# A quarter of the experts' gate and up weights multiplied as whole float32, with the output scaling on ScalarE and the factor row on GpSimd

## The chip, the cores and the metric

The kernel runs on one core of a Trainium2 chip. The metric is the device time of one execution in microseconds (us). Lower is better.

## The reference

The program is a stack of two blocks on 1024 tokens of width 1024. The first block holds a layer of dilated attention beside a gated scan and a layer of gated scans. The second holds a mixer and, last, a layer of 16 experts in which each expert chooses its tokens. The change touches only the experts:

```python
def expert_choice_ffn(h, router_w, w_gate, w_up, w_down):
    b, T, D = h.shape
    cap = EC_CAPACITY * T // N_EXPERTS
    aff = jax.nn.softmax(jnp.einsum('btd,de->bte', h.astype(F32), router_w.astype(F32)), axis=-1)
    gate, idx = lax.top_k(jnp.swapaxes(aff, 1, 2), cap)
    xe = jax.vmap(lambda hb, ib: hb[ib])(h, idx)
    hid = jax.nn.silu(jnp.einsum('becd,edf->becf', xe, w_gate)) * jnp.einsum('becd,edf->becf', xe, w_up)
    ye = jnp.einsum('becf,efd->becd', hid, w_down) * gate[..., None].astype(h.dtype)
    return jax.vmap(lambda ib, yb: jnp.zeros((T, D), yb.dtype).at[ib.reshape(-1)].add(yb.reshape(-1, D)))(idx, ye)
...
        x = x + m_lat[5][:, None] * expert_choice_ffn(h_lat, router_w[l], exp_w_gate[l], exp_w_up[l], exp_w_down[l])
```

With a capacity of 2, 1024 tokens and 16 experts, `cap` is 128 tokens. An expert's three weight matrices are 1024x512, 1024x512 and 512x1024 in float32. `m_lat[5]` is a row of 1024 factors, the same for every token; `gate` is a number per token and expert.

## The kernel before

Large products are made as three products of a reduced float32 type, `float32r`. A float32 operand is split into `hi` (its copy in float32r, by ScalarE, called ACT in the profile) and `lo` (what is left, by a subtraction on VectorE, DVE, or on GpSimd, POOL). `mm3` (L134 to L141) then issues hi x hi (L139), hi x lo (L140) and lo x hi (L141) into one bank of PSUM on TensorE (PE).

`experts` (L2002) goes through the 16 experts. For each one:

- `gather` (L2025) finds the 128 tokens by small products with a one-hot matrix, and fetches their rows with an indirect DMA that GpSimd issues (`xe`, L2041).
- `hidden` (L2049) turns the rows with eight transposes on TensorE (L2055), splits the result into `xeh` and `xel` (L132 on ACT and L133 on DVE, four chunks of 128 rows at a time), and multiplies with the gate and the up weights.
- `down` (L2071) turns and splits the hidden values (`hidh`, `hidl`), multiplies with the down weights, scales by `gate` (a number per token) and by `m5` (the factor row) in one DVE instruction per half of 512 columns (L2086), and adds the result to `accd` in DRAM with an indirect DMA from GpSimd (L2088, experts 0 to 13). The last two experts' results stay on the chip and are added by matmuls.

Each weight matrix comes in four units of 128x1024 float32 (512 KB) through `units` (L2009): a DMA from the SyncE queue into `eraw` (27 buffers in all), `ehi` by ACT (L2017), `elo` by DVE (L2019) or by POOL (L2021). `ehi` and `elo` have four buffers each. POOL makes `elo` of every unit of expert 0 and, for experts 1 to 14, of the fourth unit of each matrix; DVE makes the others. In the gate and up matrices a unit holds two chunks of 128 rows, in the down matrix one.

```python
if u < 3 and e > 0 or e == 15:
    nc.vector.tensor_sub(lo, raw, hi.bitcast(F32))
else:
    nc.gpsimd.tensor_tensor(lo, raw, hi.bitcast(F32), op=ALU.subtract)
```

The loop computes `hidden` of expert e ahead of `down` of expert e-1. What order the instructions have on each engine is decided by a scheduler when the program is built, which interleaves the two; on the chip each engine takes its instructions in that order.

## Time and profile before

| | us |
|---|---|
| three runs of the kernel | 3703.40, 3707.62, 3709.96 (median 3707.62) |
| the profiled execution, its own time | 3706.74 |
| its span, first to last instruction | 3704.5 |
| mean granted TensorE clock, share of full speed | 0.933 |
| PE busy | 3335.8 (90%) |
| DVE busy | 2592.7 (70%) |
| ACT busy | 1600.5 (43%) |
| POOL busy | 1445.3 (39%) |

Busy time is the time in which at least one instruction of the engine was running; matmuls overlap, so a busy PE can still run below its best rate. PEld is the loading of the stationary operand. A row of the trace names a source line, an engine, an operation and `out<-in`, with the number of instructions after an x. "idle before" is the time that the engine stood still ahead of these instructions, and what ended it. The experts run from about 3296 us to the end of the span; the tanh of their hidden values (L2067), one per expert, comes first at 3305.03 and last at 3654.20 us.

### The profile page before, as it was taken

How to read it: one execution, taken by the hardware profiler on the slowest of the kernel's cores; microseconds unless marked ns; L12 is line 12 of the kernel's file. 1: busy time of each engine (PE TensorE's matmuls, PEld its weight loads, DVE VectorE, ACT ScalarE, POOL GpSimd, SP SyncE). 2: the span in 40 equal slices, each digit the busy share in tenths (PEclk: the TensorE clock that was granted, in tenths of full speed). 3: DMA queues.
4: the chain of work that ended last, by engine and by line, in shares of the span. 5: the costliest groups of instructions: out<-in, count | busy, mean ns of one | idle time of the engine just before them, and what ended most of it. 6: DMA issues, size and time to landing. Idle time of an engine off the chain costs nothing.

```text
span 3704.5 us, 59873 instructions
## 1 busy us (share of the span) xinstructions
PE 3335.8 (90%) x21896; PEld 2717.0 (73%) x21896; DVE 2592.7 (70%) x5580; ACT 1600.5 (43%) x3332; POOL 1445.3 (39%) x1431
## 2 busy tenths in 40 slices
PE   7998998999979999999999999688996889748887
PEld 6886786766758888879798977566775877536665
DVE  4776664346685767976767685679995555578887
ACT  3343333544424545445545441354433331225565
POOL 4556673000041334333334331723215562335544
PEclk9998999999999999999999999788996879869999
DMA  5223244252352212111112234234337555678994
GB/s 179 78 83 95 86 134 136 79 184 88 91 170 66 70 63 57 51 56 46 46 49 65 64 135 154 76 90 130 113 117 175 119 150 177 212 210 291 302 331 161
DMA packets 373986, 461.04 MB, mean 124 GB/s; under 512 B 150419, under 2 KB 280723, under 8 KB 373692
## 3 DMA queue, kind: packets, MB, share of 16 engines
q1 hardware_dynamic: 359852, 407.93, 35.3%
q0 software_dynamic: 13840, 49.29, 4.4%
q8 instruction: 173, 2.83, 0.3%
q14 instruction: 121, 0.99, 0.1%
HBM read 357.57 MB, written 104.27 MB: 125 GB/s over the span
## 4 chain that ended last, share of the span: by engine, by line
PE 60%; DVE 16%; issue 8%; DMA 7%; POOL 4%; ACT 3%; SPq 1%; DVEq 0%; POOLq 0%; ACTq 0%
PE mm L139 12%; PE mm L140 12%; PE mm L141 11%; PE a L247 2%; DVE elo L2019 2%; PE o L225 1%; DVE cacc L1141 1%; PE a L402 1%; PE a L141 1%; PE a L140 1%; PE f L1099 1%; PE o L276 1%; POOL aw L962 1%; PE a L139 1%; PE a L251 1%
## 5 line engine op out<-in xcount | busy, mean ns | idle before, releaser
L116 POOL TENSOR_TENSOR wlo<-wraw,whi 128x1024 fp32r<-128x1024 f32 (+1 forms) x131 | 328.2, 2510 | 518.3 <-ACT whi L115 496.0
L2017 ACT CAST ehi<-eraw 128x1024 fp32r<-128x1024 f32 x192 | 200.5, 1050 | 147.2 <-PE a L141 101.8
L139 PE MATMUL mm<-x1h,whi 128*128 128x512 f32 x576 | 237.4, 412 | 7.6 <-DVE q L621 3.8
L140 PE MATMUL mm<-x1l,whi 128*128 128x512 f32 x576 | 234.9, 408 | 3.0 <-DVE x1l L133 3.0
L141 PE MATMUL mm<-x1h,wlo 128*128 128x512 f32 x576 | 234.7, 407 | 0.0
L139 PE MATMUL mm<-whi,x1h 128*128 128x256 f32 x768 | 222.4, 290 | 0.0
L2019 DVE TENSOR_TENSOR elo<-eraw,ehi 128x1024 fp32r<-128x1024 f32 x138 | 198.2, 1470 | 32.6 <-ACT ehi L2017 32.4
L141 PE MATMUL mm<-whi,x1l 128*128 128x256 f32 x768 | 219.9, 287 | 0.0
L140 PE MATMUL mm<-wlo,x1h 128*128 128x256 f32 x768 | 219.9, 287 | 0.0
L115 ACT CAST whi<-wraw 128x1024 fp32r<-128x1024 f32 (+1 forms) x131 | 136.0, 1040 | 165.1 <-PE mm L140 90.4
L2021 POOL TENSOR_TENSOR elo<-eraw,ehi 128x1024 fp32r<-128x1024 f32 x54 | 139.6, 2591 | 158.1 <-ACT ehi L2017 135.3
L139 PE MATMUL mm<-whi,xh 128*128 128x256 f32 x640 | 184.9, 289 | 0.0
L140 PE MATMUL mm<-wlo,xh 128*128 128x256 f32 x640 | 183.9, 288 | 0.5 <-POOL wlo L116 0.5
L141 PE MATMUL mm<-whi,xl 128*128 128x256 f32 x640 | 183.4, 287 | 0.0
L139 PE MATMUL mm<-x2h,whi 128*128 128x512 f32 x400 | 166.4, 416 | 6.5 <-ACT cu L1130 3.5
L139 PE MATMUL mm<-whi,yin 128*128 128x512 f32 x352 | 148.6, 425 | 22.3 <-DVE z L820 13.9
L140 PE MATMUL mm<-x2l,whi 128*128 128x512 f32 x400 | 164.7, 412 | 0.0
L141 PE MATMUL mm<-x2h,wlo 128*128 128x512 f32 x400 | 163.8, 410 | 0.8 <-POOL wlo L116 0.8
L139 PE MATMUL mm<-xh,whi 128*128 128x512 f32 x336 | 138.9, 413 | 19.8 <-ACT whi L115 16.6
L239 POOL TENSOR_TENSOR u_qh<-u_qa,facX 128x256 f32<-128x256 f32 x64 | 71.4, 1115 | 202.1 <-DVE u_qa L236 170.9
L139 PEld LDWEIGHTS mm<-whi,x1h 128*128 128x128 f32 x768 | 146.9, 191 | 1.1
L962 POOL TENSOR_SCALAR aw<-aw,ac 128x128 f32<-128x128 f32 x256 | 116.3, 470 | 80.2 <-DMA aw<-in_ada_w_dram 32.5
(755 smaller groups left out, 10700.9 us busy)
## 6 DMA issues: line engine op xcount, KB each, us to landing
eraw<-in_we_gate_dram SPq DMA_DIRECT2D x64, 512.0 KB
eraw<-in_we_up_dram SPq DMA_DIRECT2D x64, 512.0 KB
eraw<-in_we_down_dram SPq DMA_DIRECT2D x64, 512.0 KB
yin<-yd POOLq DMA_DIRECT2D x29, 1024.0 KB, 8.5
aw<-in_ada_w_dram SPq DMA_DIRECT2D x96, 256.0 KB
yd<-y_hl SPq DMA_DIRECT2D x80, 256.0 KB
wraw<-in_w_dram SPq DMA_DIRECT2D x25, 512.0 KB
wraw<-in_w_out_dram SPq DMA_DIRECT2D x24, 512.0 KB
```

The lines of the kernel that those rows point to most:

```text
L115: nc.scalar.copy(hi[:, :sz], raw[:, :sz])
L116: nc.gpsimd.tensor_tensor(lo[:, :sz], raw[:, :sz], hi[:, :sz].bitcast(F32), op=ALU.subtract)
L139: nc.tensor.matmul(ps, sh, mh, start=first and i == 0, stop=False)
L140: nc.tensor.matmul(ps, sh, ml, start=False, stop=False)
L141: nc.tensor.matmul(ps, sl, mh, start=False, stop=last and i == n - 1)
L225: nc.tensor.matmul(up[:, :Vd], kdT[:, i * P:(i + 1) * P], V[:, gi, :], start=True, stop=True)
L239: nc.gpsimd.tensor_tensor(v3(qh, 32), v3(qa, 32), bcast(fqh, nck, 32), op=ALU.mult)
L247: nc.tensor.matmul(ap[:, o:o + P], w(kt, 0, P), w(qt, 0, P), start=True, stop=True)
L962: nc.gpsimd.tensor_scalar(w[:, k], w[:, k], at(k), 0.0, op0=ALU.mult, op1=ALU.add)
L2017: nc.scalar.copy(hi, raw)
L2019: nc.vector.tensor_sub(lo, raw, hi.bitcast(F32))
L2021: nc.gpsimd.tensor_tensor(lo, raw, hi.bitcast(F32), op=ALU.subtract)
```

## The change

Of every gate and every up matrix the fourth unit (chunks 6 and 7 of 8) is no longer split. `raw` itself is the moving operand of one plain float32 matmul per chunk, against a float32 copy of the tokens' chunks 6 and 7 (`xew`). The down matrices stay as they were. For experts 0 to 13 the scaling by `gate` moves from DVE to ACT (two activations that read PSUM), and the product with the factor row `m5` becomes an instruction of its own on POOL, ahead of the indirect DMA that adds the result to `accd`.

```diff
--- before.py
+++ after.py
@@ -2006,14 +2006,18 @@
     nc, I = g.nc, g.I
     turns = cycle(rps)
 
-    def units(blk, e, k, n):
+    def units(blk, e, k, n, plain=0):
+
         out = []
         for u in range(4):
             rp, bufs = next(turns)
             raw = rp.tile([P, 1024], F32, name="eraw", tag="eraw", bufs=bufs)
+            nc.sync.dma_start(raw.rearrange("p (k n) -> p k n", n=n), blk[:, u * k:(u + 1) * k, :])
+            if u >= 4 - plain:
+                out += [raw[:, i * n:(i + 1) * n] for i in range(k)]
+                continue
             hi = wp.tile([P, 1024], F32R, name="ehi", tag="ehi", bufs=4)
             lo = wp.tile([P, 1024], F32R, name="elo", tag="elo", bufs=4)
-            nc.sync.dma_start(raw.rearrange("p (k n) -> p k n", n=n), blk[:, u * k:(u + 1) * k, :])
             nc.scalar.copy(hi, raw)
             if u < 3 and e > 0 or e == 15:
                 nc.vector.tensor_sub(lo, raw, hi.bitcast(F32))
@@ -2021,6 +2025,14 @@
                 nc.gpsimd.tensor_tensor(lo, raw, hi.bitcast(F32), op=ALU.subtract)
             out += [(hi[:, i * n:(i + 1) * n], lo[:, i * n:(i + 1) * n]) for i in range(k)]
         return out
+
+    def product(ps, sta, mov):
+
+        whole = [i for i, m in enumerate(mov) if not isinstance(m, tuple)]
+        parts = [i for i, m in enumerate(mov) if isinstance(m, tuple)]
+        g.mm3(ps, [sta[i] for i in parts], [mov[i] for i in parts], last=False)
+        for i in whole:
+            nc.tensor.matmul(ps, sta[i], mov[i], start=False, stop=i == whole[-1])
 
     def gather(e):
 
@@ -2049,19 +2061,24 @@
 
         xh = pool.tile([P, 8, P], F32R, name="xeh", tag="xeh", bufs=2)
         xl = pool.tile([P, 8, P], F32R, name="xel", tag="xel", bufs=2)
+        xw = pool.tile([P, 2, P], F32, name="xew", tag="xew", bufs=2)
         for c0 in range(0, 8, 4):
             tr = g.psum("tr")
             for i in range(4):
                 nc.tensor.transpose(tr[:, i * P:(i + 1) * P], xe[:, (c0 + i) * P:(c0 + i + 1) * P], g.ident)
+            t3 = tr.rearrange("p (c t) -> p c t", t=P)
+            m = min(4, 6 - c0)
             with g.up():
-                g.split(xh[:, c0:c0 + 4], xl[:, c0:c0 + 4], tr.rearrange("p (c t) -> p c t", t=P))
-        sta = [(xh[:, k], xl[:, k]) for k in range(8)]
-        wg = units(I["we_gate"][e], e, 2, 512)
+                g.split(xh[:, c0:c0 + m], xl[:, c0:c0 + m], t3[:, :m])
+                if c0 == 4:
+                    nc.scalar.copy(xw, t3[:, 2:4])
+        sta = [(xh[:, k], xl[:, k]) for k in range(6)] + [xw[:, k] for k in range(2)]
+        wg = units(I["we_gate"][e], e, 2, 512, 1)
         pg = g.psum("a")
-        g.mm3(pg, sta, wg)
-        wu = units(I["we_up"][e], e, 2, 512)
+        product(pg, sta, wg)
+        wu = units(I["we_up"][e], e, 2, 512, 1)
         pu = g.psum("a")
-        g.mm3(pu, sta, wu)
+        product(pu, sta, wu)
         hid = pool.tile([P, 512], F32, name="hid", tag="hid", bufs=2)
         with g.up():
             nc.scalar.activation(hid, pg, AF.Tanh, scale=0.5)
@@ -2083,8 +2100,12 @@
             hs = slice(half * 512, (half + 1) * 512)
             pd = g.psum("o")
             g.mm3(pd, [(hh[:, k], hl[:, k]) for k in range(4)], [(h[:, hs], l[:, hs]) for h, l in wd])
-            nc.vector.scalar_tensor_tensor(y[:, hs], pd, gate, m5[:, hs], op0=ALU.mult, op1=ALU.mult)
+            if e < 14:
+                nc.scalar.activation(y[:, hs], pd, AF.Copy, scale=gate)
+            else:
+                nc.vector.scalar_tensor_tensor(y[:, hs], pd, gate, m5[:, hs], op0=ALU.mult, op1=ALU.mult)
         if e < 14:
+            nc.gpsimd.tensor_tensor(y, y, m5, op=ALU.mult)
             nc.gpsimd.indirect_dma_start(out=accd, out_offset=bass.IndirectOffsetOnAxis(ap=idx, axis=0), in_=y,
                                          in_offset=None, bounds_check=T - 1, compute_op=ALU.add)
             return
```

What the scheduler makes of it is shown at three places. The first is POOL in the middle of the experts, about one expert long. `xe<-h2d,idx` is the gather of an expert's rows, `accd<-ye,idx` the indirect add. Before:

```order
L2088 DMA accd<-ye,idx 1024x1024
L2041 DMA xe<-h2d,idx 128x1024
L2021 TENSOR_TENSOR elo<-eraw,ehi 128x1024 x3
L2088 DMA accd<-ye,idx 1024x1024
L2041 DMA xe<-h2d,idx 128x1024
```

and with the change:

```order
L2025 TENSOR_TENSOR elo<-eraw,ehi 128x1024
L2108 TENSOR_TENSOR ye<-ye,m_32846 128x1024
L2109 DMA accd<-ye,idx 1024x1024
L2053 DMA xe<-h2d,idx 128x1024
L2025 TENSOR_TENSOR elo<-eraw,ehi 128x1024
```

Between two gathers three subtractions have become one, that of the down matrix, and the product of `ye` with the factor row (L2108) stands ahead of each indirect add.

The second place is ACT late in the experts, over one expert, from the tanh (`hid<-a`) to the next. Before:

```order
L2067 ACTIVATE hid<-a 128x512
L2017 CAST ehi<-eraw 128x1024 x9
L132 CAST xeh<-tr 128x512 x2
L2017 CAST ehi<-eraw 128x1024 x2
L132 CAST hidh<-tr 128x512
L2017 CAST ehi<-eraw 128x1024
L2067 ACTIVATE hid<-a 128x512
```

and with the change:

```order
L2084 ACTIVATE hid<-a 128x512
L2021 CAST ehi<-eraw 128x1024 x6
L2104 ACTIVATE ye<-o,gate 128x512 x2
L132 CAST xeh<-tr 128x512
L132 CAST xeh<-tr 128x256
L2074 COPY xew<-tr 128x256
L2021 CAST ehi<-eraw 128x1024 x4
L2084 ACTIVATE hid<-a 128x512
L132 CAST hidh<-tr 128x512
L2021 CAST ehi<-eraw 128x1024 x5
L2104 ACTIVATE ye<-o,gate 128x512 x2
```

The twelve casts of weight units have become ten, and the two scalings of `ye` (L2104), which need the whole down product, stand ahead of the split of the next expert's tokens.

The third place is PE at the end of one expert's up product, with the change only; `a` is the bank of the gate or up product and `o` that of the down product.

```order
L139 MATMUL a<-ehi,xeh 128x512
L140 MATMUL a<-elo,xeh 128x512
L141 MATMUL a<-ehi,xel 128x512
L2035 MATMUL a<-eraw,xew 128x512 x2
L139 MATMUL o<-ehi,hidh 128x512
L140 MATMUL o<-elo,hidh 128x512
L141 MATMUL o<-ehi,hidl 128x512
```

The two float32 matmuls of the unsplit unit (L2035) close the product, where before six matmuls of L139 to L141 stood.

## Rows read from the trace of the kernel before

**Rows 1.** Stretches of the expert stage: busy time of each engine, clock, DMA.

```profile
core 0: us, PE busy (x) PEld busy (x) DVE busy (x) ACT busy (x) POOL busy (x), PEclk, DMA share, GB/s
3303.70:3353.10 49.40, 38.55 (x172) 29.55 (x171) 40.78 (x42) 27.16 (x32) 30.72 (x14) 0.90 0.71 243
3353.10:3477.40 124.30, 103.55 (x453) 79.31 (x453) 96.29 (x108) 71.45 (x78) 71.10 (x25) 0.90 0.90 289
3477.40:3654.20 176.80, 157.04 (x721) 121.25 (x721) 157.31 (x168) 116.24 (x129) 90.16 (x39) 0.97 0.86 289
```

**Rows 2.** Waits in 3300 to 3665 us: total, times, longest us.

```profile
PE a L140 <- POOL elo L2021: 15.8, 4, 5.9
PE a L140 <- DVE elo L2019: 13.0, 6, 4.6
PE a L141 <- DVE xel L133: 12.1, 7, 2.3
```

**Rows 3.** Waits of SyncE's DMA queue from 3170 us: total, times, longest us.

```profile
SPq L2016 <- DVE elo L2019: 132.9, 88, 6.9
```

**Rows 4.** Timeline around 3400 us: start, us, engine, line.

```profile
3396.01 4.72 POOL L2088 DMA_INDIRECT accd<-ye,idx  x1 [1.69 <-DVE gate L2045]
...
3401.03 4.40 POOL L2041 DMA_INDIRECT xe<-h2d,idx  x1 [0.31 <-issue]
...
3405.46 2.35 POOL L2021 TENSOR_TENSOR elo<-eraw,ehi 128x1024 fp32r<-128x1024 f32 x1
...
3407.86 0.79 PE L140 MATMUL a<-elo,xeh 128*128 128x512 f32 x1 [4.88 <-POOL elo L2021]
```

**Rows 5.** Stretches right behind the three longest such waits, columns as in rows 1.

```profile
3407.86:3412.25 4.39, 4.39 (x11) 3.46 (x11) 0.69 (x1) 1.62 (x2) 0.69 (x1) 0.51 1.04 371
3434.32:3439.50 5.18, 5.18 (x12) 4.12 (x13) 0.97 (x2) 2.09 (x2) 1.47 (x1) 0.50 0.99 364
3461.15:3466.80 5.65, 5.65 (x13) 4.46 (x14) 0.69 (x1) 2.03 (x2) 1.95 (x1) 0.50 0.82 293
```

**Rows 6.** Timeline of the early experts around 3335 us.

```profile
3333.06 7.02 POOL L2021 TENSOR_TENSOR elo<-eraw,ehi 128x1024 fp32r<-128x1024 f32 x3
...
3334.78 6.39 DVE L2019 TENSOR_TENSOR elo<-eraw,ehi 128x1024 fp32r<-128x1024 f32 x1 [0.99 <-ACT ehi L2017]
...
3341.22 0.79 PE L140 MATMUL a<-elo,xeh 128*128 128x512 f32 x1 [4.05 <-DVE elo L2019]
```

**Rows 7.** Timeline of PE around 2460 us, with a plain float32 product of 512 columns.

```profile
2459.77 0.39 PE L139 MATMUL mm<-x2h,whi 128*128 128x512 f32 x1
2460.00 1.88 PE L1149 MATMUL tr<-cu,blockones 128*128 128x512 f32 x4
```

**Rows 8.** Groups of instructions from 3300 to 3665 us: busy us, mean ns, idle before.

```profile
L2017 ACT CAST ehi<-eraw 128x1024 fp32r<-128x1024 f32 x187 | 195.5, 1050 | 131.0 <-PE a L141 101.8 <-PE o L141 15.8 <-issue 8.7
...
L2067 ACT ACTIVATE hid<-a 128x512 f32<-128x512 f32 x16 | 9.6, 600 | 8.7 <-PE a L141 8.7
...
L2086 DVE SCALAR_TENSOR_TENSOR ye<-o,gate,m 128x512 f32<-128x512 f32 x28 | 19.9, 737 | 0.6 <-PE o L141 0.6
```

**Rows 9.** Timeline of the step from one expert to the next around 3555 us.

```profile
3553.99 1.03 PE L2055 MATMUL tr<-ident,xe 128*128 128x128 f32 x8
...
3555.82 0.51 PE L139 MATMUL a<-ehi,xeh 128*128 128x512 f32 x1 [0.79 <-ACT xeh L132]
...
3556.18 1.40 DVE L2086 SCALAR_TENSOR_TENSOR ye<-o,gate,m 128x512 f32<-128x512 f32 x2
...
3558.28 0.50 PE L141 MATMUL a<-ehi,xel 128*128 128x512 f32 x1 [1.73 <-DVE xel L133]
```

**Rows 10.** Timeline around 3522 us, one subtraction on POOL and DVE beside it.

```profile
3522.04 2.41 POOL L2021 TENSOR_TENSOR elo<-eraw,ehi 128x1024 fp32r<-128x1024 f32 x1 [6.54 <-ACT ehi L2017]
...
3522.46 2.00 DVE L2045 TENSOR_TENSOR gate<-fi,picked 128x1 f32<-128x1 f32 x1
```

**Rows 11.** The instruction that makes `gate`: duration ns min/median/max.

```profile
L2045 DVE TENSOR_TENSOR gate<-fi,picked x14: 141/144/2301, 3306.4 to 3612.0; 128x1 f32<-128x1 f32 x14
```

## The prediction

> **What bounds the kernel now.** I first read the stretches of the expert stage, cut at the tanh of experts 0, 2, 7 and 15 [rows 1]. The stage has no engine that is full: PE is busy 78%, 83% and 89% of the three stretches, DVE 83%, 77% and 89%. An expert takes 124.3 / 5 = 24.9 us in the second stretch and 176.8 / 8 = 22.1 us in the third. The DMA engines are busy 0.71 to 0.90 of the time, but the queue that loads weights stands waiting for DVE's subtraction to free a raw buffer, 132.9 us in total [rows 3]. So the loads wait for the compute, not the other way round.
>
> Next I asked what PE waits for. Three kinds make 40.9 us: 15.8 us for a lower part made by POOL, 13.0 us for one made by DVE, 12.1 us for the lower part of the tokens [rows 2]. The timeline shows how the first kind comes about: on POOL an indirect add of 4.72 us and a gather of 4.40 us stand ahead of a subtraction of 2.35 us, and PE stands 4.88 us until it ends [rows 4]. Nearly all of the 15.8 us is three such waits, the longest 5.9 us, all in the second stretch. Right behind each, PE runs at a granted clock of 0.5, the lower of its two levels (1.2 GHz), after it had stood idle [rows 5].
>
> The second kind, early in the stage, is a lockout: POOL runs three subtractions in 7.02 us, and a DVE subtraction beside it takes 6.39 us and ends with POOL's last, while PE waits 4.05 us [rows 6]. The same shows on a single number: the DVE instruction that makes `gate` lasts 0.144 us as a median, but 2.00 us when it starts inside a POOL subtraction, to whose end it runs [rows 10, 11]. DVE instructions that read PSUM, such as the old scaling, never stretch (mean 737 ns over 28) [rows 8].
>
> **The change part by part.**
>
> *The float32 matmuls.* Sixteen experts x 2 matrices x 2 chunks = 64 plain products take the place of 192 reduced ones. Two plain products of 512 columns are four records in the trace and last 1.88 us; a reduced one starts 0.23 us after the last and is recorded as 0.39 us long, so 0.16 us is its tail [rows 7]. Without that tail a plain product occupies PE for (1.88 - 0.16) / 2 = 0.86 us, against 3 x 0.23 = 0.70 us. That is +0.16 us each, **+10.2 us** in all; with the tail counted, +0.24 us and +15.4 us, the upper bound. The lower bound is 0, if all of it falls into time in which PE waits now. I take +10.2, since the tail overlaps the next matmul everywhere in that row.
>
> By the Trainium skill's page FP8 and Floating Point Precision (TensorE Precision Notes) a true FP32 product takes four passes through the array. At 0.23 us a pass that would be 0.92 us, +14 us in all and a forecast of 3697; the row gives 0.86 us, so I stay with it.
>
> *The split work that goes.* Two casts of 1.05 us leave ACT per expert [rows 8] and two subtractions leave POOL (DVE in expert 15). No product of a gate or up matrix waits for POOL any more, except in expert 0. The three long waits [rows 4, 5] were of just this kind, so the 15.8 us go. What is late next is DVE's lower part for the same product: I leave 3 x 0.75 us for that, a short wait. **-13.5 us**, between 0 (the wait moves, see the rivals) and -15.8.
>
> *The clock behind them.* The three stretches hold 11, 12 and 13 matmul records in 15.2 us; at 0.23 us each they would need 8.3 us [rows 5, 7]. **-6.9 us** if PE no longer idles there, 0 if it does.
>
> *The start.* POOL makes ten lower parts for expert 0 instead of twelve, and none for the gate and up matrices of expert 1. The lockout of three POOL subtractions in a row [rows 6] shrinks by one or two. The two waits there are 4.6 us (the longest of its kind [rows 2]) and 4.05 us [rows 6]; I take off half, **-4 us**, between 0 and -8.6.
>
> *The scaling.* DVE loses 28 instructions of 0.74 us; ACT gains as many, of about 0.60 us, the price of a tanh over the same 128x512 from PSUM [rows 8]. Per expert ACT gets 2 x 0.60 and a copy of the tokens' last quarter (under 0.60 us), less two casts of 1.05: it does not grow. But the pair waits for the end of the down product, and behind it on ACT stand the casts of the next gate units and the split of the next tokens, on which PE waits first. Before, at that step PE stood 0.79 us for the split on ACT and 1.73 us for DVE, which did the old scaling ahead of it [rows 9]. The order shows one scaling, at times also one cast, now ahead of the split on ACT, and nothing ahead of it on DVE: the second scaling (0.60) and a cast (1.05) against 1.40 us of DVE. I take **0**, with bounds of -12.1 us (all waits for the token split go) and 14 x 1.65 = +23 us.
>
> *The factor row.* POOL gets 14 products of 128x1024, in place of 28 subtractions of the same size: 2.41 us each [rows 10]. They delay the indirect add, for which nothing waits until the end, and the gather behind it, whose rows are used an expert later; cover is one expert's 22 us. If that cover were gone, each gather would cost PE up to 2.41 us. I take **0**; the bound above is the last rival. Its two operands lie in SBUF, like a subtraction's.
>
> *The queue of loads.* An unsplit raw buffer comes free when PE has used it, not when DVE has. That delays two of twelve buffers by a few us with 27 in hand: **0**.
>
> The sum: 10.2 - 13.5 - 6.9 - 4 = -14.2 us on the profiled execution's 3706.7 us, 3692.5. The median of the runs is 0.9 us above that execution, so I forecast **3693 us**.
>
> **The rivals.**
>
> *Better: all of PE's waits go.* If DVE's relief empties all three kinds [rows 2], the sum is 10.2 - 40.9 - 6.9 = -37.6, about **3670 us**. For it: DVE is busy 89% of the last stretch and loses 1.5 us of instructions per expert and two lockouts. Against it: with four buffers of upper and lower parts, cast, subtraction and product still follow one another. Chance 0.10.
>
> *Even: the wait moves to the down product.* Its fourth unit is still POOL's, and now stands behind factor product, add and gather: 2.41 + 4.72 + 4.40 + 2.35 = 13.9 us after the scaling [rows 4, 10]. PE has some 36 reduced and 4 plain matmuls plus transposes to do before it needs it, 8.3 + 3.4 + 1.0 = 12.7 us, and nine down matmuls, 2.1 us. If add and gather keep stretching as in rows 4 it comes late, the waits and the low clock stay, and only the start improves: 3706.7 + 10.2 - 4 + 0.9 = **3714 us**. It decides from the point where the POOL chain passes 15 us. Against it: the third stretch has adds and gathers too, but none of those long waits, which all lie before 3467 us [rows 5]. Chance 0.17.
>
> *Slower: the factor product locks out DVE.* It starts at the end of the scaling, just when the next expert's gate units need their lower parts from DVE. If every one of the 14 holds a DVE subtraction for its 2.41 us, as the POOL subtraction held `gate` [rows 10], and PE waits for it, the price is 14 x 2.41 = 33.7 us: 3692.5 + 33.7 + 0.9 = **3727 us**. It decides from the point where PE catches up with its four buffers inside those 2.41 us. For it: after each down product the buffers are empty, PE having just used them. Against it: POOL had three such instructions per expert before (the subtractions) and has two now. Chance 0.17.
>
> The Trainium skill states the rule behind that in SBUF – State Buffer (SBUF: two separate sides): DVE with two SBUF inputs and GpSimd share one port pair, whoever starts first keeps it for the whole instruction. The rows on `gate` agree (2.00 us instead of 0.144).
>
> **How the numbers follow.** The forecast has the remaining chance, 0.56; its own range, with the start between 0 and -8.6, the plain product up to +15.4 and one or two short waits either way, is 3682 to 3703. The better case gets 0.10, even 0.17, slower 0.17. The range of 3672 to 3718 takes in the even case, half of what lies between the forecast and the slower case, and most of the better one; about 0.2 lies outside. About 0.2%, 7.4 us, is what a measurement of this kernel can tell from no change: faster means below 3700, slower above 3715. Faster: nearly all of the forecast (0.52) and the better case, 0.62. Same: the rest of the forecast and most of the even case, 0.20. Slower: 0.18.
>
> **What would show it.** PE waits for POOL's lower part in the gate and up products gone from the list after expert 0, and the second stretch, 24.9 us an expert, down to about 22; the granted clock there up from 0.90 to above 0.93. Plain records of PE in the experts, 128 in all, starting 0.43 us apart. The third stretch near 22 us an expert as before. POOL products of `ye` of about 2.4 us with DVE subtractions stretched beside them. The forecast is wrong if PE's waits in the expert stage do not fall by 15 us or more, if down products wait for POOL, or if the step between experts takes over 2.5 us of waiting.

## The result and the profile after

| | before | after |
|---|---|---|
| median of the runs measured side by side, us | 3705.59 (4 runs) | 3656.36 (4 runs, 3644.89 to 3657.66) |
| ratio to before, 95% interval | 1 | 0.9859 [0.9836, 0.9881] |
| profiled execution, its own time, us | 3706.74 | 3656.70 |
| its span, us | 3704.5 | 3654.9 |
| first to last tanh of the experts, us | 349.2 | 300.4 |

The change is faster by 49 us, about 1.4%, and lies below the forecast range of 3672 to 3718. The last line of the table says where: of the 49.6 us that the span lost, 48.8 lie between the first and the last tanh of the expert stage (from the starts of these sixteen ACT instructions in the timeline). Here is that stage in the profile after, cut at the tanh of the same experts 0, 2, 7 and 15 as [rows 1]; columns as there.

```profile
core 0: us, PE busy (x) PEld busy (x) DVE busy (x) ACT busy (x) POOL busy (x), PEclk, DMA share, GB/s
3303.10:3334.09 30.99, 30.99 (x145) 22.07 (x144) 23.45 (x32) 20.59 (x28) 19.25 (x8) 1.00 0.91 334
3334.09:3432.05 97.96, 96.69 (x446) 70.42 (x443) 90.58 (x106) 67.65 (x85) 46.70 (x21) 1.00 1.02 372
3432.05:3603.46 171.41, 160.03 (x690) 115.80 (x689) 131.41 (x153) 108.52 (x137) 67.85 (x31) 0.97 0.88 302
```

The cut of before by the starts of the tanh is 48.1, 124.3 and 176.8 us. So the stretches lost 17.1, 26.3 and 5.4 us. In the first two PE now hardly stands, its clock is 1.00 instead of 0.90, and an expert of the second takes 19.6 us instead of 24.9. POOL's busy time there fell from 71.1 to 46.7 us. PE's waits in the stage, to set beside [rows 2]:

```profile
PE a L139 <- ACT xeh L132: 6.9, 4, 1.9
PE a L140 <- DVE elo L2023: 4.3, 3, 2.0
PE a L141 <- DVE xel L133: 1.1, 1, 1.1
```

All three old kinds shrank, not only the one for POOL: 15.8 to none, 13.0 to 4.3, 12.1 to 1.1. One kind grew: the wait for the upper part of the tokens (`xeh`) was 3.2 us before (four times 0.8) and is 6.9 now. All but 1.2 us of the waits listed lie after 3500 us, in the last five experts.

Groups of instructions (busy us, mean ns). The first line is from before, 3300 to 3665 us, and goes with [rows 8]; the others are from after, 3300 to 3605 us:

```profile
L2019 DVE TENSOR_TENSOR elo<-eraw,ehi 128x1024 fp32r<-128x1024 f32 x136 | 195.8, 1474 | 32.6 <-ACT ehi L2017 32.4
...
L2023 DVE TENSOR_TENSOR elo<-eraw,ehi 128x1024 fp32r<-128x1024 f32 x130 | 176.6, 1381 | 43.7 <-ACT ehi L2021 43.3
...
L2108 POOL TENSOR_TENSOR ye<-ye,m 128x1024 f32<-128x1024 f32 x14 | 36.4, 2598 | 47.5 <-ACT ye L2104 47.5
...
L2104 ACT ACTIVATE ye<-o,gate 128x512 f32<-128x512 f32 x28 | 17.7, 687 | 0.1
```

And the plain products, in PE's timeline:

```profile
3437.40 1.88 PE L2035 MATMUL a<-eraw,xew 128*128 128x512 f32 x4
3438.71 0.80 PE L140 MATMUL o<-elo,hidh 128*128 128x512 f32 x1
```

DVE's subtractions for the lower parts have a mean of 1.38 us instead of 1.47; one that nothing stops takes 1.21 to 1.22 (the medians of the two stages). Four records of plain products last 1.88 us, to the digit what [rows 7] gave. The scaling takes 0.69 us on ACT (0.60 was taken), the factor product 2.60 us on POOL (2.41 was taken).

### The profile page after: what moved, and what is told of

It is laid out like the page before. It is cut to its first block, busy times and chain, and to the rows that moved or that the text cites. A ratio compares the mean times of both kernels' runs of the same rounds, so it can differ in the third digit from the quotient of the medians.

```text
span 3654.9 us, 59671 instructions
## 1 busy us (share of the span) xinstructions
PE 3334.1 (91%) x21832; PEld 2701.3 (74%) x21832; DVE 2541.0 (70%) x5550; ACT 1581.6 (43%) x3344; POOL 1389.0 (38%) x1415
## 4 chain that ended last, share of the span: by engine, by line
PE 65%; DVE 14%; issue 6%; DMA 6%; POOL 4%; ACT 3%; SPq 2%; DVEq 0%; POOLq 0%; ACTq 0%
PE mm L139 12%; PE mm L140 12%; PE mm L141 12%; PE a L247 2%; PE o L225 2%; PE a L2035 1%; PE a L402 1%; DVE cacc L1141 1%; PE a L140 1%; PE a L141 1%; PE a L139 1%; PE f L1099 1%; PE o L276 1%; POOL aw L962 1%; PE a L251 1%
## 5 line engine op out<-in xcount | busy, mean ns | idle before, releaser
L139 PE MATMUL mm<-x1h,whi 128*128 128x512 f32 x576 | 237.3, 412 | 7.6 <-DVE q L621 3.8
L141 PE MATMUL mm<-x1h,wlo 128*128 128x512 f32 x576 | 234.6, 407 | 0.0
L139 PE MATMUL mm<-whi,x1h 128*128 128x256 f32 x768 | 222.4, 290 | 0.0
L141 PE MATMUL mm<-whi,x1l 128*128 128x256 f32 x768 | 220.0, 287 | 0.0
L2023 DVE TENSOR_TENSOR elo<-eraw,ehi 128x1024 fp32r<-128x1024 f32 x136 | 183.9, 1374 | 46.8 <-ACT ehi L2021 46.5
L2021 ACT CAST ehi<-eraw 128x1024 fp32r<-128x1024 f32 x160 | 165.7, 1052 | 98.3 <-PE o L141 36.9
L139 PE MATMUL mm<-whi,xh 128*128 128x256 f32 x640 | 185.0, 290 | 0.0
L141 PE MATMUL mm<-whi,xl 128*128 128x256 f32 x640 | 183.5, 287 | 0.0
L139 PE MATMUL mm<-x2h,whi 128*128 128x512 f32 x400 | 166.6, 417 | 8.4 <-ACT cu L1130 5.5
L139 PE MATMUL mm<-whi,yin 128*128 128x512 f32 x352 | 148.4, 424 | 22.6 <-DVE z L820 14.1
L141 PE MATMUL mm<-x2h,wlo 128*128 128x512 f32 x400 | 164.3, 411 | 0.8 <-POOL wlo L116 0.8
L139 PE MATMUL mm<-xh,whi 128*128 128x512 f32 x336 | 139.0, 414 | 18.8 <-ACT whi L115 16.2
L139 PEld LDWEIGHTS mm<-whi,x1h 128*128 128x128 f32 x768 | 146.9, 191 | 1.1
L140 PEld LDWEIGHTS mm<-wlo,x1h 128*128 128x128 f32 x768 | 146.9, 191 | 0.8
L141 PEld LDWEIGHTS mm<-whi,x1l 128*128 128x128 f32 x768 | 146.9, 191 | 0.4
```

The costliest lines, as they stand in the source:

```text
L139: nc.tensor.matmul(ps, sh, mh, start=first and i == 0, stop=False)
L140: nc.tensor.matmul(ps, sh, ml, start=False, stop=False)
L141: nc.tensor.matmul(ps, sl, mh, start=False, stop=last and i == n - 1)
L2021: nc.scalar.copy(hi, raw)
```

## The experiments

Three theories stood against each other. A: the plain units did it, since they pass by the four buffers of upper and lower parts. B: DVE's relief from the scaling did it. C: the subtractions that left POOL had held up DVE's, as [rows 6, 10, 11] show, and PE through them. A run's name is that of its expectation. Every median stands beside the ratio to the kernel before on the same chip.

**plain_only**: the scaling goes back.

```diff
-            if e < 14:
-                nc.scalar.activation(y[:, hs], pd, AF.Copy, scale=gate)
-            else:
-                nc.vector.scalar_tensor_tensor(y[:, hs], pd, gate, m5[:, hs], op0=ALU.mult, op1=ALU.mult)
+            nc.vector.scalar_tensor_tensor(y[:, hs], pd, gate, m5[:, hs], op0=ALU.mult, op1=ALU.mult)
         if e < 14:
-            nc.gpsimd.tensor_tensor(y, y, m5, op=ALU.mult)
```

> The change with its plain units kept and its scaling undone: DVE scales by the gate and by the factor row in one instruction again, and GpSimd has no factor product. Theory A (the plain units did it: two of an expert's twelve units need no upper and lower part, so less passes through the four buffers, and PE has two stretches of about 1.7 us per expert in which the parts of the next units are made): nearly all of the gain stays, 3650 to 3668 us, and the nine tanh steps of experts 2 to 10 stay near 19.2 us. Theory B (DVE's relief from the scaling did a good half): 28 DVE instructions of about 0.74 us come back and with them PE's waits for DVE, 3675 to 3695 us, steps of 20.5 us and more. Theory C (the subtractions that left GpSimd did it, since they no longer hold DVE up): as theory A or a few us better, since the factor product goes as well, 3645 to 3660 us.

3654.64 us, 0.9896 [0.9866, 0.9925]: by the medians the time of the changed kernel (3656.36), by the ratios three quarters of its gain (0.9859), with intervals that overlap. The steps from tanh to tanh are 19.0 to 19.3 us for experts 3 to 10. B falls; A and C both had this time. The moved scaling is worth nothing that these runs can tell from noise, in either direction.

**scaling_only**: the same edit the other way, on the kernel before.

> The kernel before with only the scaling moved: by the gate on ScalarE from PSUM, by the factor row on GpSimd (experts 0 to 13); all twelve units of an expert are still split. Theory A (plain units): no gain, GpSimd has a product more per expert ahead of the add and the gather: 3700 to 3725 us. Theory B (DVE's relief): about half of the gain, 3675 to 3690 us, with the waits for DVE's lower parts (13.0 us before) mostly gone. Theory C (GpSimd's hold on DVE): slower, 14 more GpSimd instructions of 2.4 us beside DVE: 3715 to 3740 us.

3711.77 us, 1.0031 [1.0011, 1.0051]: slower by 4 to 19 us. PE's waits in its expert stage show by what:

```profile
PE a L140 <- DVE elo L2019: 30.2, 12, 4.3
PE o L140 <- DVE elo L2019: 11.6, 8, 1.7
```

DVE has 28 instructions less than before, and PE waits for it 41.8 us instead of 17.6 (13.0 [rows 2] and 4.6 for the down product). What grew is POOL's load, one product per expert. That is C's sign in the waits. The time alone does not decide: it lies in A's range and just below C's 3715 to 3740.

**no_pool_low**: the kernel before, in which the fourth gate and up units of experts 1 to 14 have no lower part. Their upper part is multiplied in its place, so PE and ACT do as much as before, and POOL's subtraction is left out.

```diff
-            lo = wp.tile([P, 1024], F32R, name="elo", tag="elo", bufs=4)
+            if not (u == 3 and k == 2 and 0 < e < 15):
+                lo = wp.tile([P, 1024], F32R, name="elo", tag="elo", bufs=4)
...
+            if u == 3 and k == 2 and 0 < e < 15:
+                lo = hi
-            if u < 3 and e > 0 or e == 15:
+            elif u < 3 and e > 0 or e == 15:
```

> The kernel before, in which the fourth unit of each gate and up matrix of experts 1 to 14 has its lower part replaced by its upper part: GpSimd's subtraction for it is left out, PE's work and ScalarE's casts are as before. Theory C (GpSimd's subtractions held DVE and PE up): most of the gain without any plain product, 3655 to 3675 us, the second stretch at 21 us an expert or less. Theory A (plain units): the waits for GpSimd's lower part and the clock behind them go, the other waits stay, 3685 to 3700 us, since the unit still takes a buffer of upper parts and PE has no stretch that needs no parts. The prediction's own sum for this part, 13.5 + 6.9 + 4 us less, would give 3681.

3657.78 us, 0.9895 [0.9865, 0.9925]: as much as plain_only, with no plain product and no scaling moved. A falls, which had 3685 to 3700. Steps of experts 3 to 8 are 18.1 to 18.7 us; those of experts 1 and 2 are 19.5 and 23.6, where the changed kernel has 12.8 and 18.2 (here expert 0 keeps all twelve lower parts on POOL). Against the changed kernel it loses 12 us in these two and makes up 7 in the others, where it pays for no plain product.

**pool_back**: the changed kernel with POOL's load given back.

```diff
                 out += [raw[:, i * n:(i + 1) * n] for i in range(k)]
+                if 0 < e < 15:
+                    junk = wp.tile([P, 1024], BF16, name="junk", tag="junk", bufs=1)
+                    nc.gpsimd.tensor_tensor(junk, raw, raw, op=ALU.subtract)
```

> The changed kernel, in which GpSimd makes a difference of 128x1024 that nobody uses for each plain unit of experts 1 to 14: its load is as before the change and more (two such instructions and the factor product per expert). PE, DVE and ScalarE have the work of the changed kernel. Theory A (plain units): 3656 to 3668 us, steps of 19.2 to 20 us. Theory C (GpSimd's hold on DVE): the gain goes, 3685 to 3705 us, with DVE subtractions stretched beside GpSimd's and PE waiting behind them.

3684.39 us, 0.9951 [0.9928, 0.9974]. More than half of the gain goes, though nobody waits for the two differences; the time ends just under C's range. PE's waits for DVE's lower parts are 17.2 us, where the changed kernel has 4.3 and the kernel before 17.6 over both kinds of product.

**plain_pool3**: the same three lines in plain_only, so that POOL has three elementwise instructions per expert, as before (an unused difference takes 1.89 us where nothing stops it, a subtraction 2.41).

> The kernel of plain_only (plain units, scaling on DVE, no factor product), in which GpSimd makes a difference of 128x1024 that nobody uses for each plain unit of experts 1 to 14. GpSimd then has three subtractions per expert, exactly as in the kernel before, but PE waits for only one of them. Theory C1 (GpSimd's instructions hold up DVE's, and through them PE): most of the gain over the kernel before goes; plain_only measured 3654.6, so this one 3680 to 3697 us, with DVE's subtractions at a mean of 1.45 us or more instead of 1.23. Theory C2 (what counted was that PE waited for the lower part from GpSimd's queue, which here is gone): 3654 to 3668 us.

3682.18 us, 0.9943 [0.9926, 0.9959], as C1 said. Against plain_only this is 28 us by the medians and 17 by the ratios.

**low_left_busy**: the same unused difference in no_pool_low.

> no_pool_low, in which GpSimd makes an unused difference of 128x1024 where the left-out subtraction was: GpSimd is as busy as in the kernel before, PE's products are those of the kernel before, but no gate or up product waits for GpSimd (the fourth units' lower part is replaced by their upper part). It splits no_pool_low's gain into the wait and the hold-up of DVE. By the sums so far (plain_pool3 against plain_only: the hold-up is worth 27 us) it comes to about 3657.8 + 27 = 3685 us, 3676 to 3692, so that PE's wait for GpSimd's lower part and the clock behind it are worth about 18 us, as the prediction's 13.5 + 6.9 had it. If it was the wait alone: 3655 to 3668. If the hold-up alone: 3695 to 3706.

3696.26 us, 0.9989 [0.9974, 1.0003], above the 3676 to 3692 expected. So PE's wait for POOL's lower part, taken away without the load on POOL, is worth 6 us by the medians and 10 at most by the interval, not 18. PE's waits there say why:

```profile
PE a L140 <- DVE elo L2024: 15.9, 9, 5.3
PE a L141 <- DVE xel L133: 14.3, 7, 2.7
```

The two kinds were 25.1 us before [rows 2] and are 30.2 now, so part of the 15.8 us came back under other names. The rest of no_pool_low's gain, 38 us by the medians (35 by the ratios) between this kernel and no_pool_low, is what the unused differences cost.

**pool_memset**: pool_back with fills in place of the difference.

```diff
-                    junk = wp.tile([P, 1024], BF16, name="junk", tag="junk", bufs=1)
-                    nc.gpsimd.tensor_tensor(junk, raw, raw, op=ALU.subtract)
+                    junk = wp.tile([P, 512], F32, name="junk", tag="junk", bufs=1)
+                    for _ in range(4):
+                        nc.gpsimd.memset(junk, 0.0)
```

> The changed kernel, in which GpSimd fills a tile of 128x512 with zeros four times for each plain unit of experts 1 to 14, in place of the unused difference of pool_back: GpSimd is busy for a similar time, but reads no operand. If GpSimd's queue being busy is what costs (its add, gather and lower part of the down weights come later), the time is near that of pool_back, 3675 to 3690 us. If what costs is that an elementwise instruction of GpSimd with operands in SBUF holds up DVE's, the time stays near that of the changed kernel, 3655 to 3668 us, and no DVE subtraction beside a fill is longer than 1.3 us. If a fill holds DVE as well, DVE's subtractions stretch to the end of each fill, by a smaller piece each: 3662 to 3685 us.

3658.65 us, 0.9878 [0.9861, 0.9894]. But this run doesn't settle what it was made for: the fills depended on nothing, and POOL had done them all by 3400 us, before most of the stage. **fill_spread** mends that with one line ahead of the fills:

```diff
+                    nc.gpsimd.tensor_copy(junk[:, :1], raw[:, :1])
```

> pool_memset once more, since there the fills waited for nothing and GpSimd had done them all by 3400 us. Here one number of the plain unit is copied ahead of its four fills of 128x512, so they run when the unit has landed, spread over the stage as the unused differences of pool_back are. Theory C1 (an elementwise instruction of GpSimd with two operands in SBUF holds up DVE's): 3652 to 3665 us, as the changed kernel, since DVE's instructions beside a fill were 1.21 us as elsewhere in pool_memset. If GpSimd's queue being busy costs by itself (the add, the gather and the down lower part start later): 3672 to 3690 us, near pool_back's 3684.

3658.27 us, 0.9874 [0.9858, 0.9891], with fills up to 3561 us, through most of the stage. A busy queue on POOL costs nothing that shows in these times. One doubt stayed: the scheduler decides PE's order anew for each program, and those of pool_back and fill_spread differ. early_busy and early_fill, below, take it away.

**dve_low**: the kernel before, with the fourth gate and up units' lower part on DVE.

```diff
-            if u < 3 and e > 0 or e == 15:
+            if (u < 3 or k == 2) and e > 0 or e == 15:
```

> The kernel before, with one edit: the lower part of the fourth unit of each gate and up matrix of experts 1 to 14 is made by DVE instead of GpSimd. No plain product, no factor product, scaling on DVE; DVE gets 28 subtractions of about 1.2 us more. Theory C (GpSimd's subtractions held DVE and PE up): faster than the kernel before although DVE has more to do, 3655 to 3680 us, with steps of 18.6 to 20 us in experts 3 to 8 as in no_pool_low where DVE keeps up. Theory B (DVE's load is the bound of the stage): slower than before, 3700 to 3730 us.

3674.94 us, 0.9922 [0.9903, 0.9942]. DVE gets two subtractions more per expert and the kernel is 28 us faster. The steps of experts 3 to 12 are 19.2 to 19.9 us.

**plain_turn**: plain_only with the tokens turned earlier in the program.

```diff
-            hid = hidden(e, at[e][0])
+            hid = hidden(e, sta)
+        if e < 15:
+            sta = turn(at[e + 1][0])
         if e > 0:
             down(e - 1, prev, *at[e - 1][1:])
```

> The kernel of plain_only, in which the program turns the tokens of expert e+1 ahead of the down product of expert e-1 instead of behind it, so that the order on PE has the down product's 24 reduced products, or the last gate and up products, between the transposes and the first product that needs their split. In the changed kernel experts 11 to 15 take 19 to 26 us each, with PE waiting 1.7 to 2.0 us for the split right behind the transposes and running at the lower clock level behind that. If that order is what makes the late experts slower than the early ones (19.2 us), they fall to 19.2 to 20 us: 3654.6 less 12 to 20 us, 3632 to 3643 us. If the late experts are slow for another reason (GpSimd's add and gather, loads), the time stays within 5 us of 3654.6.

3687.46 us, 0.9963 [0.9946, 0.9979]: a miss, 33 us slower than plain_only by the medians and 25 by the ratios. Each expert from 4 to 13 now takes 22 to 24 us. PE's waits:

```profile
PE o L141 <- DVE idx L2051: 14.9, 11, 1.5
PE o L139 <- ACT hidh L132: 5.9, 12, 0.5
```

Eleven and twelve times, so in nearly every expert, the down product now starts right behind the transposes of the hidden values, and waits for their split. On DVE a one-hot instruction of 2.25 us stands ahead of it; the list names the short `idx` behind the split. The one-hot itself is stopped: it takes 1.21 us at its shortest, and here it starts (3460.48 us) inside a subtraction on POOL that runs from 3459.29 to 3461.65. The exposed wait went from one place to another.

**early_plain**: plain_only again, with work put behind both kinds of transposes. Tokens are gathered one expert earlier, into a third buffer, for which one raw buffer goes.

```diff
-            at[e + 1] = gather(e + 1)
+            at[e + 2] = gather(e + 2)
...
         product(pg, sta, wg)
+        turned = between()
         wu = units(I["we_up"][e], e, 2, 512, 1)
...
+        if e < 15:
+            sta = turn(at[e + 1][0])
         if e > 0:
-            down(e - 1, prev, *at[e - 1][1:])
+            down(e - 1, turned, *at[e - 1][1:])
```

(`between` turns and splits the hidden values of expert e-1.)

> The kernel of plain_only with the program written in another order: the tokens of expert e+2 are gathered while expert e is computed (three buffers for them, 26 raw buffers in place of 27), the hidden values of expert e-1 are turned and split ahead of expert e's up product, the tokens of expert e+1 ahead of the down product of e-1. On PE's order, other products then stand between every group of transposes and the first product that needs its split, in the late experts too; plain_turn had covered the tokens' split only and left the split of the hidden values uncovered. If uncovered splits are what makes the late experts slow: 19.2 to 20 us for each of experts 3 to 14, 3632 to 3645 us. If the late experts are slow for another reason: 3650 to 3665 us.

3641.04 us (3632.82 to 3641.89), 0.9825 [0.9806, 0.9844]: better than the changed kernel, whose lowest run is 3644.89, though the two intervals touch. Here is one stretch of 231 us of its stage, from expert 2 into expert 14, with the columns of [rows 1]:

```profile
3323.64:3555.00 231.36, 231.36 (x1068) 171.73 (x1067) 195.87 (x263) 153.07 (x180) 74.47 (x36) 1.00 1.02 381
```

PE is busy for all of it at full clock. An expert takes 19.0 us in the middle of the stage and 18.5 to 19.5 in experts 11 to 14, where the changed kernel has 22 to 26. Only expert 15 is slower, 26.0 us against 19.3.

**early_dve**: the same order for dve_low.

> The same order for the kernel of dve_low: all units split, DVE makes the lower parts of the fourth gate and up units, no plain product, scaling on DVE. dve_low measured 3674.9 with steps of 19.9 us in experts 3 to 11 and 24 to 26 us in the last ones. If its early steps are bound by DVE (9 + 2 subtractions of 1.2 us, splits, scaling), they stay at 19.9 and only the last ones gain: 3652 to 3664 us. If they were bound by PE's waits at the splits, they fall towards the 18.5 us of no_pool_low: 3635 to 3650 us, and the float32 products would not be needed at all.

3653.02 us, 0.9866 [0.9849, 0.9883]. A stretch of 230 us in its stage:

```profile
3320.00:3550.00 230.00, 211.32 (x1013) 161.62 (x1011) 230.00 (x264) 158.98 (x176) 79.33 (x33) 1.00 0.99 346
```

Now DVE is the full engine, and an expert takes 21.0 us. Eleven lower parts take 15.5 us of it; at the 1.21 us of an undisturbed one they would take 13.3. So some 2 us of the 21.0 (an estimate) are stops beside the one subtraction per expert that POOL still makes. In dve_low, the same work in the old order, DVE is full too, at 19.9 us. With eleven lower parts and these stops DVE can't keep up, with nine it can.

**early_busy** and **early_fill**: early_plain with pool_back's difference, and with fill_spread's fills. Their orders on PE differ at two places in sixteen experts.

> early_plain, in which GpSimd makes an unused difference of 128x1024 for each plain unit of experts 1 to 14. The orders of pool_back and fill_spread on PE were not the same, since the scheduler decides them anew for each program; with this order of the program PE's order of early_busy and early_fill differs at two places among 16 experts. If GpSimd's subtractions hold up DVE and PE through it: 3641 + 20 to 30 us, 3658 to 3675 us, and above early_fill by 15 us or more. If the difference between pool_back and fill_spread was one of order: early_busy and early_fill agree within 5 us, both 3638 to 3650.

> early_plain, in which GpSimd copies one number of each plain unit of experts 1 to 14 and fills a tile of 128x512 four times: GpSimd is as busy as in early_busy, but its fills read nothing. Hold-up of DVE as the cause: 3638 to 3648 us, as early_plain. GpSimd's busy queue as the cause: near early_busy, 3658 to 3675 us.

3675.15 us, 0.9931 [0.9903, 0.9959], and 3645.11 us, 0.9851 [0.9815, 0.9886]. The two differ by 30 us, with the same work on PE, DVE and ACT and nearly the same order. DVE's lower parts from 3295 to 3660 us (busy us, mean ns), first with the difference, then with fills:

```profile
L2026 DVE TENSOR_TENSOR elo<-eraw,ehi 128x1024 fp32r<-128x1024 f32 x136 | 215.7, 1619 | 22.3 <-ACT ehi L2024 22.2
...
L2028 DVE TENSOR_TENSOR elo<-eraw,ehi 128x1024 fp32r<-128x1024 f32 x136 | 167.5, 1254 | 38.4 <-ACT ehi L2026 38.3
```

The timelines of POOL, DVE's lower parts and PE's waits, first with the difference:

```profile
3437.77 1.22 DVE L2026 TENSOR_TENSOR elo<-eraw,ehi 128x1024 fp32r<-128x1024 f32 x1
...
3439.94 7.64 DVE L2026 TENSOR_TENSOR elo<-eraw,ehi 128x1024 fp32r<-128x1024 f32 x3 [0.35 <-ACT ehi L2024]
...
3439.95 2.41 POOL L2028 TENSOR_TENSOR elo<-eraw,ehi 128x1024 fp32r<-128x1024 f32 x1
...
3442.34 1.89 POOL L2020 TENSOR_TENSOR junk<-eraw 128x1024 bf16<-128x1024 f32 x1
...
3445.36 0.50 PE L140 MATMUL a<-elo,xeh 128*128 128x512 f32 x1 [1.28 <-DVE elo L2026]
```

then with fills:

```profile
3439.57 2.27 POOL L2022 MEMSET junk<- 128x512 f32 x4
3439.64 1.23 DVE L2028 TENSOR_TENSOR elo<-eraw,ehi 128x1024 fp32r<-128x1024 f32 x1 [0.18 <-ACT ehi L2026]
...
3441.03 1.23 DVE L2028 TENSOR_TENSOR elo<-eraw,ehi 128x1024 fp32r<-128x1024 f32 x1 [0.17 <-ACT ehi L2026]
```

Three DVE subtractions take 7.64 us beside two POOL instructions of 4.30 us, and 1.22 us each elsewhere: 3 x 1.22 + 4.30 = 7.96, so DVE stands nearly as long as POOL runs. Beside four fills a DVE subtraction takes its usual 1.23 us.

Not all that an unused difference costs lies in the stage. From the first to the last tanh the profiled executions differ by 25 us here (316.9 against 291.5), by 23 and 26 for pool_back and plain_pool3 against their partners, and by 33 for low_left_busy against no_pool_low. The rest lies ahead of the first tanh, where the differences for expert 1 already run; what it is was not looked into.

**early_split**: the kernel before in the order of early_plain, POOL making its lower parts.

> The kernel before (all units split, GpSimd makes the lower part of each fourth unit, scaling on DVE) with the program order of early_plain. It tells what the order is worth without the change. If GpSimd's subtractions hold up DVE whatever the order is: 3685 to 3705 us, at most 15 us better than the kernel before, DVE's subtractions at a mean of 1.4 us or more. If the waits came from the order: 3650 to 3670 us, near early_dve's 3653.

3670.91 us, 0.9918 [0.9895, 0.9942], far below the 3685 to 3705 of the hold-up and at the edge of the 3650 to 3670 of the order. DVE's subtractions still have a mean of 1.46 us, as the hold-up had it, but PE's wait for POOL's lower part in the gate and up products is 0.7 us with this order, where it was 15.8. So the order alone, without the change, is worth 30 us, and the step from here to early_plain another 30. Change and order together gain 61 us and not 49 + 30: the two overlap.

**early_half**: one plain unit per expert.

```diff
-        wu = units(I["we_up"][e], e, 2, 512, 1)
+        wu = units(I["we_up"][e], e, 2, 512, 0)
...
-        product(pu, sta, wu)
+        g.mm3(pu, sta[1], wu)
```

(The tokens are split whole for this product, and DVE makes the lower part of its fourth unit.)

> early_plain with one plain unit per expert instead of two: the gate's fourth unit is plain, the up's is split, its lower part made by DVE. PE saves two plain products per expert (0.16 us each by the prediction's price), DVE gets one subtraction of 1.2 us more. early_plain runs at 19.0 us an expert with PE full, early_dve (two more subtractions on DVE) at 21.0 with DVE full. If PE is still the bound with one: 18.7 us an expert, 3634 to 3641 us. If DVE is: 19.3 to 20.2 us, 3643 to 3655 us.

3637.64 us, 0.9841 [0.9807, 0.9875]: the same as early_plain within the measurement. Its steps are 18.7 us in experts 5 to 9, where early_plain has 19.0 to 19.1, and PE has no gap in either: two plain products of 512 columns fewer are 0.3 us, 0.15 each. DVE, with ten lower parts and the stops beside POOL, is full as well (columns as in [rows 1]):

```profile
3353.00:3485.00 132.00, 131.60 (x629) 101.86 (x628) 131.94 (x162) 97.54 (x112) 46.10 (x21) 1.00 1.03 382
```

## Why the prediction was wrong

*What bounds the kernel.* Right that no engine was full and that PE's waits were the lever. The rows that decided it were on the table too: the lockout [rows 6, 10, 11]. One reading of them was loose: the subtraction in [rows 6] ends 1.09 us behind POOL's last, about its own length. And the queue of loads waited for POOL nearly as long as for DVE, which [rows 3] leaves out:

```profile
SPq L2016 <- POOL elo L2021: 125.2, 31, 34.2
```

That wait is 57.4 us after the change. It is not what costs: it is 68.5 us in early_busy and 63.3 in early_fill, which are 30 us apart in time.

*The float32 matmuls, +10.2 us.* Right where it can be seen. The price was 0.16 us each; early_half against early_plain shows 0.15 in a stretch where PE is full, and the records are those of [rows 7]. The sentence drawn from the Trainium skill, FP8 and Floating Point Precision (TensorE Precision Notes), would have had 0.22; the rows decide for the lower one.

*The split work that goes, -13.5 us, and the clock behind it, -6.9 us.* This step failed as the prediction put it. It took the wait for POOL's lower part as a thing to be removed by itself and left 3 x 0.75 us for what is late next. low_left_busy takes that wait away, leaves the load on POOL, and gains 6 us: the waits for DVE's parts grew by 5.1 us, and the clock behind the waits did not come back (0.93 from the first to the last tanh, 0.94 before).

*The start, -4 us.* This is the term that was mis-sized, and most of the miss. It was the only place where the relief of the lockout was priced, and only at two waits of the first experts. The first stretch alone gave 17.1 us, beyond its bound of 8.6, and the relief went on through the stage. By the runs two unused differences per expert on POOL cost 17 to 38 us, whichever kernel they are put into: 17 to 28 by plain_pool3, 35 to 38 by low_left_busy, 30 by early_busy. I had the mechanism, its rows and its page, and used them for a rival that ends slower; I counted 14 products coming (33.7 us) and not 28 subtractions going at the same price. The net is 14 fewer, and at the same price the forecast would have been 3693 - 14 x 2.41 = 3659. That this comes near 3656 is luck in part: the sum would still hold the 20.4 us for the wait and its clock, of which low_left_busy shows about 6, and a stop has no fixed price. The changed kernel has 14 more such instructions on POOL than plain_only and takes the same time. Here is plain_only's second stretch, to set beside that of the changed kernel above:

```profile
3328.82:3424.82 96.00, 96.00 (x446) 70.72 (x443) 81.50 (x115) 63.36 (x75) 29.02 (x16) 1.00 1.03 383
```

DVE is busy 90.6 us of 98.0 in the one and 81.5 of 96.0 in the other, and PE is full, or nearly so, in both: DVE has room for the stops there. That a stop costs only where this room ends is read from these two lines; no run was made to show it.

*The scaling, 0.* Right: plain_only and the changed kernel don't differ. The wait that its upper bound spoke of exists, 6.9 us for `xeh` behind two scalings on ACT, but plain_only, with 4.0 us of it, has slow late experts as well (22 to 25 us).

*The even rival, 3714.* It did not come: PE waits for no lower part from POOL in the stage, in the down products either.

*The factor row, 0, and the slower rival.* In the changed kernel right by its sum, as far as plain_only, which has neither the product nor the moved scaling, can tell. The rival's mechanism shows where the order exposes it, in a late expert:

```profile
3497.50 2.42 POOL L2025 TENSOR_TENSOR elo<-eraw,ehi 128x1024 fp32r<-128x1024 f32 x1
3498.28 8.32 DVE L2023 TENSOR_TENSOR elo<-eraw,ehi 128x1024 fp32r<-128x1024 f32 x4 [1.17 <-ACT ehi L2021]
...
3502.31 3.21 POOL L2108 TENSOR_TENSOR ye<-ye,m 128x1024 f32<-128x1024 f32 x1 [2.38 <-ACT ye L2104]
...
3506.66 0.50 PE L140 MATMUL a<-elo,xeh 128*128 128x512 f32 x1 [2.00 <-DVE elo L2023]
```

Four DVE subtractions take 8.32 us around the down unit's subtraction and the factor product, and PE stands 2.00 us. The granted clock of the stretch behind it is 0.57, near the lower level, as in [rows 5]:

```profile
3506.66:3510.60 3.94, 3.84 (x9) 2.85 (x10) 0.98 (x3) 1.42 (x2) 0.00 (x0) 0.57 1.03 412
```

Where POOL still has its three subtractions, the product and the moved scaling together cost 4 to 19 us (scaling_only).

*The better rival, 3670.* It had the right picture, all of PE's waits gone through DVE's relief, but named B's relief (the scaling) next to two lockouts, and priced the clock at the three stretches of [rows 5] alone, while the clock rose from 0.90 to 1.00 over the first two stretches of [rows 1]. Its objection, that four buffers still chain cast, subtraction and product, did not hold.

*The third stretch "as before".* It gained 5.4 us net of 5.1 us of plain products. What holds it is the order: after 3490 us the tokens' transposes stand right behind the down product with nothing to cover their split. early_plain, with plain_only's work in another order, takes 18.5 to 19.5 us for experts 11 to 14, where plain_only takes 22 to 25. Its order includes the earlier gather and the third token buffer, and which part of it counts was not separated. One of the prediction's signs of being wrong came here: between 3502 and 3507 us one step holds 1.65 and 2.00 us of waiting, more than 2.5.

*What the plain units are good for.* Not for sparing PE, which pays for them, but for leaving out two subtractions that POOL could make only by stopping DVE, and DVE, beside POOL's last one, only by becoming the bound (early_dve, 21.0 us an expert). One of the two DVE can take over for nothing (early_half). The rest is argued from early_dve and early_plain together; a kernel with all twelve lower parts on DVE and none on POOL was not tried. How the DMA engines, busy at 1.02 where PE is full, would bound a still faster stage was not tried.

## What to carry to other kernels

A wait is counted under the name of what came last, and taking that one away often only shows the next. Look for what makes all of them late: here an engine whose work stopped another's, which the trace shows as one instruction of several times its usual length that ends with an instruction on the other engine, or one usual length behind it. When a mechanism is priced for what a change adds, price what it removes as well, and ask at both places whether the stopped engine has room; and before giving work to an idle engine, see whether what it runs there reads the same memory as the busy one.

## What the runs showed of the hardware

A fill on POOL doesn't hold DVE (1.23 us beside four of them), an elementwise instruction of POOL that reads its operands does (7.64 us for three). The Trainium skill says so in SBUF – State Buffer (Who interferes with whom): a DVE instruction with two inputs in SBUF contends with a GpSimd instruction that reads SBUF, not with one that only writes. The traces agree in both halves. Stops of this kind count as busy time and stand in no list of waits. By the price of the unused differences, 17 to 38 us for two per expert, they cost the kernel before more than the longest of PE's waits in the stage, 15.8 us.
